# Down projection with sums kept in PSUM banks and block sums in fixed order, and output projection begun in attention for its first column half only

## The chip, the cores and the metric

The kernel runs on one core of one Trainium2 chip. The metric is the device time of one execution in microseconds (us): three executions of the kernel before gave 2621.82, 2611.28 and 2616.64 us, median 2616.64 us. Engines are named as in the profile: PE (TensorE matmul), PEld (its weight loads), DVE (VectorE), ACT (ScalarE), POOL (GpSimd), SP (SyncE, which issues the DMAs).

## The reference, cut to what matters

Two layers on x (1024 rows, 1024 columns, float32). Each is a mixer and a feed-forward part, each with a norm before and a norm after, whose result is added to x.

```
for layer in range(2):
    h = rms_norm(x, norm_mix_pre[layer])
    if layer % 2 == 0:      # FoX heads and MLA heads, outputs concatenated
        m = even_mixer(h, ...)          # ends in  concat(fox_out, mla_out) @ w_out
    else:                   # differential attention with ALiBi
        m = odd_mixer(h, ...)           # ends in  o @ w_out
    x = x + rms_norm(m, norm_mix_post[layer])
    h = rms_norm(x, norm_ffn_pre[layer])
    gate, val = split(h @ w_up)                       # 1024 x 5632
    act = gelu(causal_depthwise_conv3(gate))
    f = (act * val) @ w_down                          # 2816 -> 1024
    x = x + rms_norm(f, norm_ffn_post[layer])
return x
```

`rms_norm(y, g) = y * rsqrt(mean(y*y) + 1e-6) * g`. The two places that the change touches are `@ w_out` (the output projection, contraction over 1024) and `@ w_down` (the down projection, contraction over 2816), with the norm behind each.

## The kernel before, in words

**Numbers.** A float32 operand is cut into a high and a low part (`split`: ACT casts the high part, L121, and DVE or POOL subtracts to get the low part, L122), and each product is three matmuls, high·high, high·low, low·high (`hl`, `mm3`, L142). Every matmul of the kernel but the transposes and a few others has line 142, so groups are told apart by their tiles.

**Order.** The text of the kernel says what is computed. A scheduler, when the kernel is built, fixes each engine's order of instructions; at run time every engine works through its own list in that order and waits on semaphores. The transposed attention output goes to memory (`oT`) and comes back as tiles `ot`. Buffers come from pools with fixed counts: X 14 (128x4x512), Q 18 (128x512), T 6 (128x1024), `raw` 2 (128x1024), WL 8 (128x512); PSUM banks are S 2, mm 2, tr 3, pv 1. A tile has to wait until a buffer of its pool is free.

**Attention and its filler.** Each attention head is a generator (`mla_head`, `diff_head`). `weave` runs a head and between its steps takes steps of a second generator, `dense`, up to a budget for each head (`MLA_DENSE`, `DIFF_DENSE`): matmuls of other work that keep PE busy while DVE, ACT and POOL do the softmax. In the MLA heads of layer 0 `dense` is first the remaining projections of MLA and then `out_first`; in layer 1 it ends in `out_first` too.

**Output projection.** The eight blocks of the contraction (k-blocks) are in two groups. `out_first` does k-blocks 0 to 3, for 8 row blocks m (7 down to 0) and both column halves n: 8 x 2 x 4 x 3 = 192 matmuls a layer, each partial sum copied by ACT to an `opart` buffer. After attention `mixer_end` runs `out_second`: k-blocks 4 to 7, another 192 matmuls, 24 for a row block, and a DVE add with the partial sum for each half (L479). Behind each row block stands the norm: Square with sum on ACT (L202 for the first half, L212 for the second), the gain on POOL (L203, L213), the reciprocal root in small steps on ACT and DVE (L156 to L160), two scalar_tensor_tensor on DVE that add to x (L216, L217), the next norm (L225, L227), transposes on PE (L235), the evacuations of the block sums for the up projection (L506 to L528), and then `ffn_up`.

**Down projection.** `ffn_down` is a 2x2 block product by the Strassen–Winograd scheme with 7 products instead of 8. Each product is `prod(an, bn, ...)`: 11 k-blocks, taken in pairs, x 4 row tiles x 3 = 132 matmuls of 128x512; 7 x 132 = 924 a layer. Of each pair it loads the left block sum (`uraw`; the sums A11, A12, A22, S1 to S4 lie in memory), loads or makes the right one, splits both, and multiplies. Right operands T1 to T4 are differences of the four blocks of the weights: B11 is kept (`dB`), T3 is kept and turned into T2 (`dT`), and `comb` (L684, DVE) makes each where the product needs it, 44 a layer. Each product starts fresh PSUM banks, in the order A11·B11, A12·B21, S3·T3, S2·T2, S1·T1, S4·B22, A22·T4, and the sums between products are DVE adds (L754, L761, L765, L766, L770, L774) and POOL adds (L762) on SBUF tiles `C`. The last product holds back its last 5 k-blocks (`TAIL`) and does them row tile by row tile, so that a row tile is finished every 15 matmuls; behind each comes the norm of its row block (`fin_a`, `post_late`), with no next norm in layer 1.

## Time and profile before

| | |
|---|---|
| median of three runs | 2616.64 us (2611.28 to 2621.82) |
| profiled execution, its own time | 2621.89 us |
| its span in the profile | 2620.1 us |
| granted PE clock, mean | 0.971 |
| PE busy / DVE / ACT / POOL of the span | 94% / 68% / 47% / 50% |
| MLA attention with its filler, layer 0 | 350 to 586 us |
| output projection's second part and norm, layer 0 | 592 to about 700 us |
| down projection, layer 0 | 1095 to 1322 us |
| differential attention, layer 1 | 1370 to 1873 us |
| output projection's second part and norm, layer 1 | 1873 to about 1980 us |
| down projection, layer 1 | 2376 to 2605 us; end of span 2620 us |

Times are us from the start of the span. In the rows of a window view the columns are the stretch, its length, then for PE, PEld, DVE, ACT and POOL the busy time with the number of instructions, then the granted PE clock (1.00 is full), the busy share of the DMA engines and GB/s. A row of waits names the waiting engine and line, what it waited for, and total us, times and the longest. A busy PE is not a PE at its peak, since the ends of matmuls are modelled; counts of matmuls tell more, and a few per cent of their records can be missing.

### The profile page before, as it was taken

The numbers are of one execution on the slowest core, as the hardware profiler recorded it, in microseconds if no ns is written. First come the engines' busy times: TensorE is split into PE (matmuls) and PEld (weight loads), VectorE is DVE, ScalarE is ACT, GpSimd is POOL, SyncE is SP. The second block draws the span as 40 slices with busy tenths as digits, with TensorE's granted clock in tenths as the row PEclk, the third lists the DMA queues.
The fourth block names the chain that finished last, engine by engine and source line by source line (L and its number), as shares of the span: only waits on it lengthen the run. The fifth ranks groups of instructions, "written<-read, shape, count | busy, mean of one in ns | idle before, by whom it ended". The sixth has DMA issues, their size and how long they took to land. (4 is left out here: it accounts for less than half of the span.)

```text
span 2620.1 us, 36572 instructions
## 1 busy us (share of the span) xinstructions
PE 2467.1 (94%) x12326; PEld 2077.1 (79%) x12326; DVE 1768.7 (68%) x3631; ACT 1234.9 (47%) x2465; POOL 1299.1 (50%) x1172
## 2 busy tenths in 40 slices
PE   9999899998799999989989999999969999999897
PEld 7888688776688888878878888987757888887686
DVE  5555788657866666666665676777686666656768
ACT  4455578664433333434445555555454333334443
POOL 3445665435577677731321323322267777776132
PEclk9999999898899999999999999999989999999999
DMA  3332333335222323574542112133442332326545
GB/s 140 91 91 77 113 82 89 97 97 169 75 105 106 108 95 111 181 242 156 173 143 57 59 56 73 57 95 103 146 140 73 109 109 93 108 105 230 184 149 213
DMA packets 172156, 307.78 MB, mean 117 GB/s; under 512 B 16936, under 2 KB 67768, under 8 KB 171968
## 3 DMA queue, kind: packets, MB, share of 16 engines
q1 hardware_dynamic: 171968, 305.44, 35.7%
q8 instruction: 98, 1.61, 0.3%
q14 instruction: 90, 0.74, 0.1%
HBM read 213.84 MB, written 76.85 MB: 111 GB/s over the span
## 5 line engine op out<-in xcount | busy, mean ns | idle before, releaser
L142 PE MATMUL psmm<-hT,whi 128*128 128x512 f32 (+1 forms) x960 | 311.6, 401 | 0.6 <-DVE qb L315 0.5
L122 POOL TENSOR_TENSOR wlo<-wraw,whi 128x512 fp32r<-128x512 f32 (+2 forms) x96 | 130.5, 1367 | 266.4 <-ACT whi L121 241.3
L351 ACT ACTIVATE t<-t,mn 128x896 f32<-128x896 f32 (+7 forms) x256 | 198.9, 777 | 127.7 <-DVE mn L343 121.1
L142 PEld LDWEIGHTS psmm<-hT,whi 128*128 128x128 f32 (+1 forms) x960 | 176.1, 190 | 34.5 <-issue 0.7
L142 PE MATMUL psmm<-hT,wlo 128*128 128x512 f32 (+1 forms) x480 | 190.1, 397 | 0.0
L121 ACT CAST d<-uraw 128x512 fp32r<-128x512 f32 x154 | 91.6, 618 | 140.8 <-DMA uraw<-uS 82.6
L142 PE MATMUL psmm<-wo,ot 128*128 128x512 f32 x576 | 146.8, 397 | 0.0
L380 PE MATMUL pstr<-ident,t 128*128 128x128 f32 x864 | 136.4, 280 | 6.4 <-DVE t L1199 2.1
L122 POOL TENSOR_TENSOR d<-uraw,d 128x512 fp32r<-128x512 f32 x66 | 100.3, 1538 | 84.6 <-ACT d L121 83.7
L142 PE MATMUL psmm<-whi,hT 128*128 128x256 f32 (+1 forms) x576 | 123.0, 301 | 9.1 <-ACT hT L247 4.3
L122 DVE TENSOR_TENSOR d<-wdraw,d 128x512 fp32r<-128x512 f32 x88 | 88.4, 1026 | 58.4 <-ACT d L121 45.3
L142 PEld LDWEIGHTS psmm<-wo,ot 128*128 128x128 f32 x576 | 105.8, 189 | 20.7 <-DVE qb L315 0.2
L610 ACT ACTIVATE y<-gate,cols 128x1024 f32<-128x1024 f32 x44 | 50.8, 1155 | 147.9 <-DVE gate L605 147.9
L142 PE MATMUL pstr<-T,S3h 128*128 128x512 f32 x352 | 112.7, 401 | 5.1 <-DVE B L507 5.1
L142 PE MATMUL psmm<-B,A12h 128*128 128x512 f32 x352 | 110.9, 396 | 5.0 <-DVE B L507 5.0
L380 PEld LDWEIGHTS pstr<-ident,t 128*128 128x128 f32 x864 | 102.9, 145 | 15.9 <-POOL t L902 3.6
L122 DVE TENSOR_TENSOR S2l<-s,S2h 128x512 fp32r<-128x512 f32 x44 | 65.1, 1480 | 74.5 <-ACT S2h L121 74.5
L385 DVE TENSOR_TENSOR ptq<-pstr,ptq 128x512 fp32r<-128x512 f32 (+1 forms) x160 | 99.5, 630 | 23.6 <-ACT ptq L384 19.3
L614 ACT ACTIVATE y<-y,cols 128x1024 f32<-128x1024 f32 x44 | 50.7, 1153 | 135.9 <-DVE y L612 135.9
L603 DVE TENSOR_TENSOR u<-u,psmm 128x512 f32<-128x512 f32 x44 | 29.9, 680 | 117.9 <-PE psmm L142 117.9
L142 PE MATMUL psmm<-B,A11h 128*128 128x512 f32 x352 | 109.3, 390 | 0.0
L142 PE MATMUL psmm<-T,S2h 128*128 128x512 f32 x352 | 108.8, 390 | 0.0
(357 smaller groups left out, 7636.4 us busy)
## 6 DMA issues: line engine op xcount, KB each, us to landing
wdraw<-in_ffn_down_dram SPq DMA_DIRECT2D x60, 512.0 KB, 4.7
wg<-in_ffn_up_dram SPq DMA_DIRECT2D x44, 512.0 KB, 3.4
wv<-in_ffn_up_dram SPq DMA_DIRECT2D x44, 512.0 KB, 3.5
uS<-us SPq DMA_DIRECT2D x88, 256.0 KB, 2.0
uraw<-uS SPq DMA_DIRECT2D x40, 512.0 KB, 4.1
uA<-y SPq DMA_DIRECT2D x66, 256.0 KB, 2.1
ot<-oT SPq DMA_DIRECT2D x64, 256.0 KB, 3.5
uraw<-uA SPq DMA_DIRECT2D x30, 512.0 KB, 4.5
```

The source lines that it names most:

```text
L121: nc.scalar.copy(R(hi), raw)
L122: lo_eng.tensor_tensor(R(lo), raw, hi, ALU.subtract)
L142: ins = nc.tensor.matmul(out, R(l), R(r), start=first and j == 0, stop=last and j == n - 1).ins
L351: nc.scalar.activation(t[:, :W], t[:, :W], AF.Exp, bias=mn, scale=-1.0, accum_out=l)
L380: nc.tensor.transpose(tp[:, c:c + P], pts[qi][:, b * P:(b + 1) * P], ident)
L385: nc.vector.tensor_tensor(R(pl[:, :c]), tp[:, :c], ph[:, :c], ALU.subtract)
L603: nc.vector.tensor_tensor(u2, s1, p6, ALU.add)
L610: nc.scalar.activation(y, gp, AF.Copy, scale=col(2, f))
L614: nc.scalar.activation(y, y, AF.Gelu_apprx_tanh, bias=cb)
```

## The change

1. **Output projection.** `out_first` does only the first column half (96 matmuls, 8 copies). `out_second` does the other half wholly: per row block 12 matmuls for n = 0 as before, and 24 for n = 1, summed in PSUM. It loads and splits the weights of k-blocks 0 to 3 for n = 1 itself and loads `ot` of these k-blocks again. The second half no longer passes a DVE add: Square reads PSUM, and its gain is a DVE multiply from PSUM to `xn`, which takes the place of POOL's L213.
2. **Budgets.** `MLA_DENSE` and `DIFF_DENSE` are lower, most in the last heads.
3. **Down projection.** The products go in the order A11·B11, A12·B21, S2·T2, S1·T1, S3·T3, S4·B22, A22·T4 and sum in PSUM: S2·T2 goes on in the banks of A11·B11, S3·T3 and A22·T4 in those too, and S4·B22 in those of S1·T1. There are 12 DVE evacuations a layer instead of 24 (and 4 gain multiplies from PSUM), 12 ACT copies instead of 8, and no POOL add.
4. **Block sums.** 11 of the 44 subtractions, those that make T2, stay where the product needs them (`comb`); the other 33 are `side` subtractions into the kept tiles, done a pair later, from loads of single 128x512 blocks into WL, each ordered on DVE behind the last split of the pair by a dependency that carries no data. In all 44 as before, with the same bytes.

```diff
-DIFF_DENSE = (29, 31, 28, 32, 30, 30, 28, 25)
+DIFF_DENSE = (27, 29, 26, 30, 28, 27, 24, 20)
-MLA_DENSE = (8, 8, 6, 6, 6, 7, 18, 18)
+MLA_DENSE = (7, 7, 6, 5, 5, 6, 7, 7)
...
-    def mm3(out, prods, first, last):
+    def mm3(out, prods, first, last, more=False):
...
-            ins = nc.tensor.matmul(out, R(l), R(r), start=first and j == 0, stop=last and j == n - 1).ins
+            ins = nc.tensor.matmul(out, R(l), R(r), start=first and j == 0, stop=last and j == n - 1, skip_group_check=more).ins
...
-    def post_late(m, n, src, sse, early, g_post, xi, xq, cut=False):
+    def post_late(m, n, src, sse, early, g_post, xi, xq, cut=False, home=None):
...
-        nc.gpsimd.tensor_tensor(src, src, g_post[n], ALU.mult)
+        if home is None:
+            nc.gpsimd.tensor_tensor(src, src, g_post[n], ALU.mult)
+        else:
+            nc.vector.tensor_tensor(home, src, g_post[n], ALU.mult)
+            src = home
...
     def out_first(w_src, oT, part):
-        w = [wo_quads(w_src, 0, n) for n in range(2)]
+        w = wo_quads(w_src, 0, 0)
...
     def out_second(w_src, oT, part, fin_0, fin_e, fin_a, fin_b, ahead):
-        w = [wo_load(w_src, 4, 0, lambda k: (buf("Q", "woh"), buf("Q", "wol"))), wo_quads(w_src, 4, 1)]
+        lo = buf("X", "wo")
+        w1 = wo_load(w_src, 0, 1, lambda k: (buf("Q", "woh"), lo[:, k, :]))
+        o1 = {7: oT_load(oT, 0, 7, "Q")}
+        w0 = wo_load(w_src, 4, 0, lambda k: (buf("Q", "woh"), buf("Q", "wol")))
+        w1 += wo_quads(w_src, 4, 1)
...
-                r = part[m // 4, n][:, m % 4, :]
-                for k in range(4):
-                    mm3(o, hl(tuple(t[:, k * P:(k + 1) * P] for t in ot[m]), w[n][k]), k == 0, k == 3)
-                nc.vector.tensor_tensor(r, r, o, ALU.add)
+                ks = ((4, 5, 6, 7) if n == 0 else (0, 1, 2, 3, 4, 5, 6, 7) if m == 7 else (4, 5, 6, 7, 0, 1, 2, 3))
+                for k in ks:
+                    src = (ot if k > 3 else o1)[m]
+                    mm3(o, hl(tuple(t[:, (k % 4) * P:(k % 4 + 1) * P] for t in src), w0[k - 4] if n == 0 else w1[k]), k == ks[0], k == ks[-1])
+                if n == 0:
+                    r = part[m // 4][:, m % 4, :]
+                    nc.vector.tensor_tensor(r, r, o, ALU.add)
+                    fin_e(m, 0, r)
+                else:
+                    r = o
...
+            side = dict(B21=((0, 1), b0, 1), T1=((0, 0), b0, 0), B22=((1, 0), t, 1)).get(name)
+            if side:
+                (k, j), dst, first = side
+                b = [buf("WL", "wdside") for _ in range(n)]
+                for i in range(n):
+                    nc.sync.dma_start(b[i], wd[k * NP + g + i, :, j * HALF:(j + 1) * HALF])
+                xy = (b, dst) if first else (t, b)
+                late.append(lambda: [nc.vector.tensor_tensor(d, x, y, ALU.subtract).ins for d, x, y in zip(dst, *xy)])
...
+                for f in side:
+                    for ins in f():
+                        tc.add_manual_dep(ins, last.name, behind, reason="order")
...
+        prod("A11", "B11", x, True)
...
+        prod("A12", "B21", y, True)
...
+        prod("S2", "T2", x, False)
         for t in range(4):
-            nc.scalar.copy(q7[:, t, :], p[t])
+            nc.scalar.copy(u2[:, t, :], x[t])
...
+        prod("S1", "T1", y, True)
...
+        prod("S3", "T3", x, False)
         for t in range(4):
-            tt(c22[:, t, :], q7[:, t, :], p[t], ALU.add)
-            tt(q1[:, t, :], q1[:, t, :], p[t], ALU.add)
+            tt(c22[:, t, :], p5[:, t, :], x[t], ALU.add)
...
+        prod("S4", "B22", y, False, wide=layer == 1)
...
+        prod("A22", "T4", x, False, [lambda t=t: fin_b(t) for t in range(4)], TAIL, layer == 1)
         for t in range(4):
-            tt(q7[:, t, :], q7[:, t, :], p[t], ALU.add)
-            fin_a(4 + t, 0, q7[:, t, :], c22[:, t, :])
+            fin_a(4 + t, 0, x[t], c22[:, t, :], p5[:, t, :])
```

In the rows below a name is the tile's name with the number of its buffer's use; a matmul's row is its output, then weights and moving operand as the profile names them.

PE, the last head of MLA attention in layer 0, before: `psS` and `pspv` are the head's scores and products with V (`mq`, `Vm`, `ptq`), `psmm<-wo,ot` is the filler, the output projection's first part.

```order
L142 MATMUL psmm_6844<-wo_5520,ot_6764 128x512
L142 MATMUL psS_6833<-mq_5341,mq_5154 128x384
L142 MATMUL psS_6833<-mq_5342,mq_5154 128x384
L142 MATMUL psS_6833<-mq_5341,mq_5155 128x384
L142 MATMUL psmm_6844<-wo_5521,ot_6764 128x512
L142 MATMUL psmm_6844<-wo_5520,ot_6766 128x512
L142 MATMUL psmm_6844<-wo_5520,ot_6764 128x512
```

PE in the change: the last filler of the same attention, and what follows it.

```order
L143 MATMUL psmm_7082<-wo_6984,ot_7001 128x512
L143 MATMUL psS_6669<-mq_5522,mq_5335 128x128
L143 MATMUL psS_6669<-mq_5523,mq_5335 128x128
L143 MATMUL psS_6669<-mq_5522,mq_5336 128x128
L143 MATMUL psmm_7082<-woh_6998,ot_7003 128x512
L385 MATMUL pstr_6562<-ident,t_6535 128x128
L385 MATMUL pstr_6562<-ident,t_6513 128x128
```

From there to the end of attention stand 126 rows of the heads without a filler, where before the filler ran into the middle of the last head. The tile `psmm_7082` is the second column half of row block 7, k-blocks 0 to 3: its 12 matmuls are all of the moved work that is still in attention; the other 84 of the 96 stand in `out_second`, 12 behind each row block:

```order
L143 MATMUL psmm_7161<-wo_7025,ot_7045 128x512
L143 MATMUL psmm_7161<-woh_6987,ot_7051 128x512
L143 MATMUL psmm_7161<-wo_6984,ot_7051 128x512
L143 MATMUL psmm_7161<-woh_6987,ot_7053 128x512
L143 MATMUL psmm_7161<-woh_6990,ot_7051 128x512
```

DVE in the down projection of layer 0, where the third product's first pairs are made ready, before (S3·T3): `d<-uraw` and `d<-dT` (L122) are splits that PE waits for, L684 the block sums, L754 the sums of the product before.

```order
L122 TENSOR_TENSOR d_11875<-uraw_11866,d_11874 128x512
L122 TENSOR_TENSOR d_11877<-dT_11322,d_11876 128x512
L684 TENSOR_TENSOR dT_11323<-wdraw_11958,wdraw_11960 128x512 x2
L684 TENSOR_TENSOR dT_11322<-dT_11322,dB_11319 128x512
L684 TENSOR_TENSOR dT_11324<-wdraw_12003,wdraw_12005 128x512 x2
L754 TENSOR_TENSOR C_11327<-C_11326,psmm_11564 128x512
L754 TENSOR_TENSOR C_11327<-C_11326,pstr_11565 128x512
L122 TENSOR_TENSOR d_11849<-uraw_11821,d_11849 128x512
L684 TENSOR_TENSOR dT_11324<-wdraw_12048,wdraw_12050 128x512
L122 TENSOR_TENSOR d_11849<-dT_11322,d_11849 128x512
```

The third product of the change (S2·T2) on the same engine, with the last block sums of the product ahead of it (L700) and the sums L787:

```order
L700 TENSOR_TENSOR dT_11333<-wdraw_12034,dB_11330 128x512 x2
L700 TENSOR_TENSOR dT_11333<-wdraw_12077,dB_11330 128x512
L122 TENSOR_TENSOR d_11867<-uraw_11860,d_11866 128x512
L122 TENSOR_TENSOR d_11869<-dT_11331,d_11868 128x512
L787 TENSOR_TENSOR C_11340<-C_11339,psmm_11574 128x512
L122 TENSOR_TENSOR d_11910<-uraw_11903,d_11909 128x512
L787 TENSOR_TENSOR C_11340<-C_11339,pstr_11575 128x512
L122 TENSOR_TENSOR d_11886<-uraw_11860,d_11886 128x512
```

No block sum stands between the splits of this product any more. The second product, A12·B21, now holds 11 splits, the 11 side subtractions (L726) and the 11 of T2 (L700).

DVE in the last rows of the program, before (L774 is the sum of the last product, L214 to L160 the root, L216 and L217 the additions to x):

```order
L774 TENSOR_TENSOR C_23942<-C_23942,psmm_25511 128x512
L159 TENSOR_SCALAR cvpost_25795<-cvpost_25795,rrpost_25796 128x1
L160 TENSOR_SCALAR rrpost_25796<-cvpost_25795,rrpost_25796 128x1
L216 SCALAR_TENSOR_TENSOR xq_25789<-C_23943,rrpost_25796,xq_25789 128x512
L217 SCALAR_TENSOR_TENSOR xq_25789<-C_23942,rrpost_25796,xq_25789 128x512
```

And in the change, where L217 is the gain multiply from PSUM and L221 and L222 are the additions:

```order
L217 TENSOR_TENSOR C_23968<-psmm_23964,gain_23950 128x512
L219 TENSOR_SCALAR ssl_25834<-ssl_25834,sse_25222 128x1
L158 TENSOR_SCALAR cvpost_25838<-ssl_25834 128x1
L159 RECIPROCAL rrpost_25839<-cspost_25840 128x1
L160 TENSOR_SCALAR cvpost_25838<-cvpost_25838,rrpost_25839 128x1
L161 TENSOR_SCALAR rrpost_25839<-cvpost_25838,rrpost_25839 128x1
L221 SCALAR_TENSOR_TENSOR xq_25832<-C_23969,rrpost_25839,xq_25832 128x512
```

The sum of the last row tile no longer stands in the chain of the row tile ahead of it; the multiply stands in its own.

More of the change, by code (lines that the diff above doesn't have):

```diff
@@ L446, in out_first @@
     def out_first(w_src, oT, part):
[L448 removed]
+        w = wo_quads(w_src, 0, 0)
         for m in range(7, -1, -1):
             ot = oT_load(oT, 0, m)
[L451 to L465 removed]
+            if m // 4 not in part:
+                part[m // 4] = buf("X", "opart")
+            o = bank("mm")
+            for k in range(4):
+                mm3(o, hl(tuple(t[:, k * P:(k + 1) * P] for t in ot), w[k]), k == 0, k == 3)
+                if k < 3:
+                    yield
+            nc.scalar.copy(part[m // 4][:, m % 4, :], o)
+            yield
+    def out_second(w_src, oT, part, fin_0, fin_e, fin_a, fin_b, ahead):
+        lo = buf("X", "wo")
[3 more added lines that the diff above has]
+        w1 += wo_quads(w_src, 4, 1)
         ot = {m: oT_load(oT, 1, m) for m in (7, 6, 5)}
+        o1[6] = oT_load(oT, 0, 6, "Q")
         fin_0(7)
@@ L470, in out_second @@
                 ot[m - 3] = oT_load(oT, 1, m - 3)
+            if m < 7 and m:
+                o1[m - 1] = oT_load(oT, 0, m - 1, "Q")
             if m:
@@ L691, in btiles, with prod @@
                 return b0
-            if name[0] == "B":
-                return bload(int(name[1]) - 1, int(name[2]) - 1, g, n)
-            if name == "T1":
-                b = bload(0, 1, g, n)
-                return comb(b, b, b0, ALU.subtract)
-            if name == "T3":
-                return comb(t, bload(1, 1, g, n), bload(0, 1, g, n), ALU.subtract)
-            if name == "T2":
-                return comb(t, t, b0, ALU.add)
-            b = bload(1, 0, g, n)
-            return comb(b, b, t, ALU.subtract)
-        def prod(an, bn, tags, between=(), tail=0, wide=True):
-            banks = [bank(t) for t in tags]
+            if name in ("T1", "T3"):
+                res = b0
+            elif name == "T4":
+                res = t
+            else:
+                res = bload(*dict(B21=(1, 0), B22=(1, 1), T2=(1, 1))[name], g, n)
+            if name == "T2":
+                return comb(t, res, b0, ALU.subtract)
+            side = dict(B21=((0, 1), b0, 1), T1=((0, 0), b0, 0), B22=((1, 0), t, 1)).get(name)
[6 more added lines that the diff above has]
+                late.append(lambda: [nc.vector.tensor_tensor(d, x, y, ALU.subtract).ins for d, x, y in zip(dst, *xy)])
+            return res
+        def prod(an, bn, banks, start, between=(), tail=0, wide=True):
             between = list(between)
-            held = []
+            held, late = [], []
             def mul(mt, g, t):
@@ L712, in mul @@
                 ms = slice(mt * P, (mt + 1) * P)
-                mm3(banks[mt], hl((ah[:, ms], al[:, ms]), (bh, bl)), g == 0, g == NP - 1)
+                mm3(banks[mt], hl((ah[:, ms], al[:, ms]), (bh, bl)), start and g == 0, g == NP - 1, not start)
             for g0 in range(0, NP, 2):
@@ L729, in prod @@
                     split(ar[:, i * HALF:(i + 1) * HALF], ah, al, nc.vector if bn[0] == "T" else nc.gpsimd)
-                    split(bt[i], bh, bl, nc.gpsimd if an == "A11" and g0 == 0 else nc.vector)
+                    last = split(bt[i], bh, bl, nc.gpsimd if an == "A11" and g0 == 0 else nc.vector)
                     if g0 + i >= NP - tail:
@@ L735, in prod @@
                             mul(mt, g0 + i, t)
+                for f in side:
+                    for ins in f():
+                        tc.add_manual_dep(ins, last.name, behind, reason="order")
                 if between:
                     between.pop(0)()
+            for f in late:
+                f()
             for mt in range(4):
@@ L743, in ffn_down @@
         names = [t for t in ("S", "pv", "mm", "tr") for _ in range(PB[t])]
-        sa, sb_ = names[:4], names[4:]
         tt = nc.vector.tensor_tensor
-        q1, c11, q7, c22 = (buf("X", "C") for _ in range(4))
-        p = prod("A11", "B11", sa)
+        x = [bank(t) for t in names[:4]]
+        q1, c11, u2, p5, c22 = (buf("X", "C") for _ in range(5))
+        prod("A11", "B11", x, True)
         for q in t3q:
@@ L1053, in fin_a @@
         def fin_a(m, n, late, early):
-            post_late(m, n, late, sse[m], early, gpost, 2 * layer, xqs[m])
+            post_late(m, n, late, sse[m], early, gpost, 2 * layer, xqs[m], home=xqs[m][1][:, :HALF])
             pre_norm_a(xqs[m], gpre)
@@ L1073, in fin_e, with fin_a @@
             sse[m] = post_early(n, src, gpost, ostage("o", bufs=2).bitcast(BF16))
-        def fin_a(m, n, late, early):
+        def fin_a(m, n, late, early, home=None):
             xqs[m] = xq_pair("X")
             x_load(m, 2 * layer + 1, xqs[m])
-            post_late(m, n, late, sse[m], early, gpost, 2 * layer + 1, xqs[m], last)
+            post_late(m, n, late, sse[m], early, gpost, 2 * layer + 1, xqs[m], last, home)
             if not last:
```

42 lines of the change are left out of this document (13 added, 29 removed).

## The prediction

> **What bounds the kernel now.** First the page's line of busy times, then windows over the stages, then PE's waits stage by stage.
>
> ```profile
> PE 2467.1 (94%) x12326; PEld 2077.1 (79%) x12326; DVE 1768.7 (68%) x3631; ACT 1234.9 (47%) x2465; POOL 1299.1 (50%) x1172
> ```
>
> PE is busy 2467.1 of the 2620.1 us, and the change neither adds nor removes a matmul. So it can only win some of the 153 us in which PE idles, or lose by adding to them. Where these lie is read stage by stage; the seven stretches that matter:
>
> ```profile
> core 0: us, PE busy (x) PEld busy (x) DVE busy (x) ACT busy (x) POOL busy (x), PEclk, DMA share, GB/s
> 350.00:586.40 236.40, 225.80 (x1397) 199.66 (x1395) 168.84 (x477) 171.92 (x396) 114.49 (x160) 0.97 0.32 88
> 500.00:560.00 60.00, 60.00 (x328) 51.32 (x327) 26.30 (x67) 32.28 (x71) 15.66 (x22) 1.00 0.25 71
> 569.50:586.40 16.90, 15.07 (x110) 13.30 (x108) 13.89 (x43) 13.14 (x32) 7.55 (x11) 1.00 0.30 85
> 1370.00:1862.00 492.00, 475.34 (x2847) 417.93 (x2846) 341.41 (x1095) 258.86 (x569) 135.12 (x188) 0.98 0.25 74
> 617.00:641.00 24.00, 24.00 (x120) 20.12 (x118) 21.59 (x45) 13.52 (x32) 18.37 (x13) 1.00 0.41 141
> 641.00:700.00 59.00, 36.24 (x141) 27.64 (x140) 49.69 (x81) 25.82 (x56) 38.80 (x25) 0.77 0.26 89
> 1922.00:1980.00 58.00, 35.08 (x140) 26.96 (x139) 48.86 (x84) 27.48 (x59) 40.44 (x26) 0.79 0.29 99
> ```
>
> Rows one to four are attention. Both attentions are bound by PE: in MLA's 236.4 us PE idles 10.6 and DVE is busy 71%, in the differential's 492 us 16.7 and 69%; where the output projection fills (500 to 560) PE never stops and DVE has 26.3 of 60. Without filler (569.5 to 586.4) PE is busy 15.07 of 16.9. Rows five to seven are the output projection's second part and the norm: PE first full with DVE at 90%, then, with the projection finished at 641 while the norms run on, PE at 60% for 59 us, in both layers.
>
> ```profile
> 1155.00:1196.00 41.00, 31.39 (x121) 25.04 (x120) 36.39 (x53) 15.78 (x32) 6.06 (x4) 0.88 0.50 170
> 1196.00:1227.00 31.00, 31.00 (x138) 25.67 (x138) 21.60 (x35) 20.44 (x38) 0.00 (x0) 1.00 0.50 165
> 2407.00:2440.00 33.00, 30.41 (x127) 24.68 (x127) 21.17 (x24) 11.85 (x23) 12.04 (x9) 0.95 0.83 292
> 2440.00:2478.00 38.00, 28.92 (x118) 23.12 (x117) 33.91 (x49) 14.55 (x31) 6.15 (x4) 0.87 0.37 128
> PE psS L142 <- DVE d L122: 11.1, 3, 6.1
> ```
>
> These are products of the down projection, 132 matmuls each, and PE's waits for splits in layer 0. S3·T3 (1155 and 2440) takes 41 and 38 us, and DVE is busy 89% of it; its neighbour S2·T2 takes 31 with PE full.
>
> **The change part by part.** The price of a matmul, from the last ones:
>
> ```profile
> 2603.97 0.84 PE L142 MATMUL psmm<-d 128*128 128x512 f32 x3
> 2604.65 0.84 PE L142 MATMUL psmm<-d,d 128*128 128x512 f32 x3
> ```
>
> Three every 0.68 us, 0.227 each.
>
> *Attention.* Of the 96 matmuls a layer that leave `out_first`, the order of PE shows 12 still inside attention, so 84 x 0.227 = 19.0 us of PE work leave each attention. PE bounds it, so at most 19.0 is won. Against that, thinner filler shows waits: of the 126 rows at MLA's end that now have none, the trace already has about 110 matmuls unfilled with 1.8 us lost per 16.9, and the shares of DVE and ACT rise to 169 and 172 of 217 us, under 80%. I charge 6 us a layer for MLA and 5 for the differential one, whose budgets fall by 1 to 5 in each head: three to four waits of 1 to 2 us. **−13 and −14.** Bounds: −19 (no new wait) and −4 (as many us of waits again as PE idles now).
>
> *Output projection's second part.* The 84 matmuls come back here: 24 a row block before, 36 now. PE then needs 36 x 0.227 + about 0.8 for transposes = 9.0 us a row block, 8 x 9.0 = 72 in all where it had 49 (592 to 641). DVE is what the stage waits for now:
>
> ```profile
> PE pstr L235 <- DVE xn L227: 11.1, 3, 7.1
> PE pspv L142 <- ACT B L506: 6.2, 1, 6.2
> 591.81 0.77 PE L142 MATMUL psS<-woh,ot 128*128 128x512 f32 x1 [5.19 <-DMA ot<-oT]
> 674.20 2.39 DVE L227 SCALAR_TENSOR_TENSOR xn<-xr,rrpre,gain 128x1024 f32<-128x1024 f32 x1
> L227 DVE SCALAR_TENSOR_TENSOR xn<-xr,rrpre,gain 128x1024 f32<-128x1024 f32 x8 | 12.6, 1578 | 0.1
> L216 DVE SCALAR_TENSOR_TENSOR xr<-opart,rrpost,xr 128x512 f32<-128x512 f32 x8 | 9.2, 1149 | 0.8 <-POOL opart L203 0.3
> ```
>
> Its row blocks go at 9 us (21.59 busy of 24, 45 instructions), and the chain of the last one ends the stage: PE's waits for `xn` of 11.1 us and for the last evacuation of 6.2. 72 us of PE fit under the 85 us after which the last `xn` is there (591.8 to 676.6 in the rows): the last row block then ends at 592 + 72 = 664, some 12 us of chain behind it (Square, root, additions, the next norm) give 676 as before, and the 59 us stretch with 23 idle is where the 19 us go. **0 in both layers**: hidden by the norms. If that cover fails, rows go at PE's pace with DVE's on top, and up to 19 us a layer come back. The DVE add L479 of 0.68 us becomes a multiply of the same size; POOL loses eight multiplies. Bounds −6 to +8 a layer; the extra loads (`ot` once more, 8 x 2 x 256 KB = 4 MB, and 1 MB of weights that moves here) are some 70 GB/s over 72 us, where DMA shares are 0.26 to 0.41.
>
> ```profile
> 604.77 1.84 DVE L217 SCALAR_TENSOR_TENSOR xr<-opart,rrpost,xr 128x512 f32<-128x512 f32 x1
> 612.38 0.75 DVE L217 SCALAR_TENSOR_TENSOR xr<-opart,rrpost,xr 128x512 f32<-128x512 f32 x1
> 604.78 1.28 POOL L203 TENSOR_TENSOR opart<-opart,gain 128x512 f32<-128x512 f32 x1 [1.25 <-ACT xn L202]
> ```
>
> The same addition takes 1.84 us when a POOL multiply starts beside it and 0.75 alone. By the Trainium skill ("SBUF — State Buffer", "Who interferes with whom") a DVE instruction with two SBUF inputs contends with a GpSimd instruction that reads SBUF, and one with at most one SBUF input does not; the rows agree, and by it every POOL multiply that leaves spares about 1 us, so that the stage would be some 4 us a layer shorter and the whole 8. I keep 0, since POOL still has its other multiply and the block sums to do beside these additions.
>
> *Down projection.* The 44 block sums stay 44, but before, 20 to 26 of them stood in S3·T3 between the splits that PE waits for (order of DVE). Dense, a product is 132 x 0.227 = 29.9 us. S3·T3 is over by 41 − 29.9 = 11.1 in layer 0; A12·B21 and S3·T3 by 3.1 and 8.1 in layer 1: 22.3 in all. Now A12·B21 has 11 splits at 1.0, 22 sums at 0.78 = 28 us of DVE, S1·T1 22 splits at 0.73 and 11 sums = 25, S2·T2 and S3·T3 22 splits and 4 sums = 19.
>
> ```profile
> L122 DVE TENSOR_TENSOR d<-wdraw,d 128x512 fp32r<-128x512 f32 x42 | 41.3, 1002 | 31.4 <-ACT d L121 29.0 <-DMA wdraw<-in_ffn_down_dram 2.4
> L122 DVE TENSOR_TENSOR d<-uraw,d 128x512 fp32r<-128x512 f32 x44 | 31.7, 730 | 18.2 <-ACT d L121 18.2
> L684 DVE TENSOR_TENSOR wdraw<-wdraw,dB 128x512 f32<-128x512 f32 x11 | 8.2, 776 | 0.0
> ```
>
> All under 29.9, A12·B21 barely. I take 17 of 22.3: **−9 and −8**; bounds −22 and −6 for both (A12·B21 late by 8 a layer). The sums moved from SBUF to PSUM banks save DVE 12 x 0.68 = 8 us a layer beside full PE: nothing. At the end of layer 0 PE waits 4.3 us for the next layer's `hT`; four sums and POOL's multiplies fewer in front of it: **−2** (−4 to +1).
>
> ```profile
> PE psmm L142 <- ACT hT L247: 4.3, 1, 4.3
> ```
>
> *The end of layer 1.* After PE's last matmul (2605.5) the last row's sum waits until the chain of the row ahead lets it in:
>
> ```profile
> 2610.19 0.67 DVE L774 TENSOR_TENSOR C<-C,psmm 128x512 f32<-128x512 f32 x1
> 2610.94 0.63 ACT L212 ACTIVATE xq<-C 128x512 f32<-128x512 f32 x1 [0.86 <-DVE C L774]
> 2611.99 1.75 DVE L217 SCALAR_TENSOR_TENSOR xq<-C,rrpost,xq 128x512 f32<-128x512 f32 x1
> 2613.67 0.20 DVE L214 TENSOR_SCALAR ssl<-ssl,sse 128x1 f32<-128x1 f32 x1
> 2614.99 0.75 DVE L216 SCALAR_TENSOR_TENSOR xq<-C,rrpost,xq 128x512 f32<-128x512 f32 x1
> 2615.65 0.75 DVE L217 SCALAR_TENSOR_TENSOR xq<-C,rrpost,xq 128x512 f32<-128x512 f32 x1
> ```
>
> It starts 4.7 us late, and the last addition ends at 2616.4, 10.9 after the last matmul; the output's DMA ends at 2620.1. Now Square (0.63, and 0.19 to read its sum), the multiply (0.68), the root (2613.67 to 2614.99 in the rows, 1.3) and two additions (0.75 each, nothing of POOL's beside them) make about 4.5 us a row; rows come every 15 x 0.227 = 3.4, so the last is up to 2 us late: 5 to 6.5 after the last matmul. **−5** (−7 to −2).
>
> *Sum.* −13 −14 + 0 −9 −8 −2 −5 = −51 on the profiled execution of 2621.9 (span 2620.1 and 1.8 around it): 2571. That execution lies 5.3 above the median 2616.6, so 2565.6 by the median, rounded to **2565**.
>
> **Rivals.** *A, the moved projection is paid back.* For: DVE is at 90% in 617 to 641 and its chain and PE's longer rows may add rather than overlap, since Square and multiply now hold a PSUM bank until both are through. Against: 23 us of idle PE right behind, in each layer. Then attention's 27 come back, 14 to 19 a layer, say 32; the rest is −24: −24 − 27 + 32 = −19, by the median 2597.
>
> *B, A12·B21 is bound by transfers.* It now loads T2's and B12's blocks beside A12 and B21; layer 1's row 2407 to 2440 already shows a DMA share of 0.83 and 3.1 us lost. Some 3 MB more at the 292 GB/s of that row are 10 us a layer, of which about 8 count; single loads of 256 KB have to issue in front of the next `uraw` on SP. Down then gives −1 in place of −17: about 2581. For: DVE's 28 of 29.9 us there. Against: the loads can start in the product before.
>
> *C, slower: the thinner fill lets PE cool.* Place: attention in both layers, at the heads' ends. The trace has such a case:
>
> ```profile
> PE pspv L142 <- DVE ptq L385: 3.3, 1, 3.3
> 480.00:490.00 10.00, 8.68 (x41) 8.20 (x42) 6.71 (x20) 4.79 (x13) 4.17 (x7) 0.66 0.33 96
> 490.00:500.00 10.00, 9.85 (x69) 8.62 (x68) 8.89 (x28) 8.43 (x20) 5.20 (x7) 1.00 0.50 148
> ```
>
> A wait of 3.3 us (to 481.3), and in the 10 us behind it a granted clock of 0.66 and 41 matmuls, then 1.00 and 69. Price: 3.3 and (1 − 0.66) x 10 = 3.4, so 6.7 us. The forecast's 51 are used up from 8 such waits over both layers; ten give −51 + 67 = +16, some 2632. Against: no single wait in the differential attention is over 2.7 us now, and DVE would have 20% of air.
>
> ```profile
> PE psS L142 <- DMA ot<-oT: 2.7, 1, 2.7
> ```
>
> By the Trainium skill ("TensorE: Matmul & The Clock Gate", "What's actually happening") the clock falls to half after an idle window of about 3.4 us and comes back after a busy one of that length. The rows agree as far as 0.66 over 10 us goes, and this speaks for C deciding by long waits only, not by many short ones.
>
> *D, little moves.* PE loses in attention what it is relieved of, the stage behind is hidden, B holds too: only the tail and some 5 of the down projection remain, −10 to −12, about 2605.
>
> **How the numbers follow.** Forecast 0.62, spread 2550 to 2584; A 0.14 (2590 to 2606); B 0.11 (2576 to 2588); D 0.08 (2600 to 2612); C 0.05 (2630 and over). A measurement of this kernel can tell about 0.5% from no change, 13 us, so faster means under 2604. Faster: the forecast, B, most of A and a part of D, 0.85; same 0.10 (rest of A, D, an edge of C); slower 0.05. The range takes in A and leaves out C and most of D, and reaches down by the better ends of attention, down projection and the stage between, −51 − 28: **2538 to 2604**.
>
> **What would show it.** Attention 350 to 586 shorter by 13, 1370 to 1862 by 14, with some 84 matmuls fewer; 592 to 700 and 1873 to 1980 equally long with 84 more and PE nearly full to 660; S3·T3 no longer over 32 us and A12·B21 not over 33; the last addition 5 to 6.5 us behind the last matmul. Wrong: a wait for `xn` as long as before behind a projection that ends 20 us later (A), a DMA share over 0.9 in A12·B21 (B), a clock under 0.9 in attention (C).

## The result, and the profile after

The changed kernel takes 2581.6 us (median of four runs, 2578.5 to 2586.6) where the kernel before took 2619.2 (2611.28 to 2625.39): ratio 0.9857, 95% interval 0.984 to 0.9875, 37.6 us less by the medians. The forecast was 2565, in a range of 2538 to 2604. The profiled execution is the shortest of the four, 2578.5 us with a span of 2576.4; against the profiled execution before the span is 43.7 us shorter.

The page's line of busy times after the change:

```profile
PE 2457.8 (95%) x12326; PEld 2072.2 (80%) x12326; DVE 1754.5 (68%) x3615; ACT 1232.3 (48%) x2457; POOL 1256.7 (49%) x1140
```

PE has the same 12326 matmuls, and its idle time has gone from 153 to 119 us; the other 9 us of the 43.7 are busy time, at a mean granted clock of 0.977 in place of 0.971. To find where, take the first matmul of each part in PE's timeline (start, length, group, what ended the idle time ahead of it), first before, then after:

```profile
1094.74 0.84 PE L142 MATMUL psS<-d,d 128*128 128x512 f32 x3
1873.38 0.76 PE L142 MATMUL psS<-woh,ot 128*128 128x512 f32 x1 [2.73 <-DMA ot<-oT]
2375.62 0.84 PE L142 MATMUL psS<-d,d 128*128 128x512 f32 x3
```

```profile
570.62 0.77 PE L143 MATMUL psS<-woh,ot 128*128 128x512 f32 x1 [6.17 <-DMA ot<-oT]
1077.92 0.84 PE L143 MATMUL psS<-d,d 128*128 128x512 f32 x3
1831.11 0.79 PE L143 MATMUL psS<-woh,ot 128*128 128x512 f32 x1 [1.65 <-DMA ot<-oT]
2335.08 0.84 PE L143 MATMUL psS<-d,d 128*128 128x512 f32 x3
2568.20 0.84 PE L143 MATMUL psmm<-d,d 128*128 128x512 f32 x3
```

`psS<-woh,ot` opens the output projection's second part, `psS<-d,d` the down projection; the last row is its last group in layer 1. With the ends of the down projection (layer 0: 1322.7 before, 1300.8 after; layer 1: 2605.5 and 2569.0), and the stretch between the layers cut at the first product of probabilities with V, they give every part of the span:

| part | before | after | difference | forecast |
|---|---|---|---|---|
| start to second part, layer 0 (attention) | 591.8 | 570.6 | −21.2 | −13 |
| second part to down projection, layer 0 | 502.9 | 507.3 | +4.4 | 0 |
| down projection, layer 0 | 227.9 | 222.9 | −5.0 | −9 |
| passage to layer 1, to its first product with V | 92.0 | 85.2 | −6.8 | −2 |
| from there to the second part, layer 1 (attention) | 458.8 | 445.0 | −13.8 | −14 |
| second part to down projection, layer 1 | 502.2 | 504.0 | +1.8 | 0 |
| down projection, layer 1 | 229.9 | 234.0 | +4.1 | −8 |
| last matmul to end of span | 14.6 | 7.4 | −7.2 | −5 |
| span | 2620.1 | 2576.4 | −43.7 | −51 |

The first row is not all the change's. The same matmul (`psS<-qb,qb` of a head ahead of MLA's, whose budget the change leaves as it was) starts at 345.40 before and at 342.33 after, and in all twelve profiled executions of this document it lies between these two; 3.1 of the 21.2 us are this spread, and 18.1 stand behind that matmul. So the attention windows below start at a common matmul: layer 0, layer 1, and the 20 us that end 5 us ahead of layer 1's second part, first before, then after:

```profile
345.40:586.40 241.00, 230.40 (x1420) 203.54 (x1418) 171.47 (x487) 173.97 (x401) 118.84 (x168) 0.97 0.32 89
1414.63:1873.38 458.75, 438.39 (x2663) 385.97 (x2663) 329.62 (x1083) 243.62 (x546) 127.38 (x182) 0.98 0.26 77
1848.40:1868.40 20.00, 18.17 (x102) 15.05 (x100) 10.83 (x46) 7.71 (x22) 0.32 (x1) 1.00 0.38 132
```

```profile
342.33:564.40 222.07, 210.67 (x1336) 185.37 (x1334) 170.02 (x488) 169.32 (x393) 120.12 (x168) 0.98 0.38 107
1386.06:1831.11 445.05, 424.18 (x2583) 376.61 (x2582) 327.99 (x1076) 240.28 (x538) 122.86 (x182) 0.96 0.28 83
1806.10:1826.10 20.00, 15.90 (x74) 13.60 (x72) 14.14 (x55) 9.46 (x27) 5.41 (x8) 0.60 0.83 277
```

In layer 0 what left is PE work (84 matmul records, 19.7 us), and the idle rest stayed: 10.6 before, 11.4 after, the clock full to the end. In layer 1 the idle rest stayed too (20.4 and 20.9), but PE's busy time fell by only 14.2 us, and its last 20 us, where the filler is thin now, ran at a clock of 0.60 and not 1.00, with 74 matmuls and not 102. No single wait of PE there is over 1.6 us. At this place the kernel before and the run below with the old output projection show 1.00, and all ten with the new one 0.60 to 0.84.

The stage behind, after:

```profile
570.60:646.80 76.20, 75.97 (x348) 62.61 (x348) 54.84 (x114) 34.19 (x81) 33.82 (x23) 0.97 0.56 182
646.80:680.00 33.20, 20.94 (x85) 16.83 (x86) 25.81 (x38) 16.03 (x29) 18.95 (x12) 0.79 0.22 72
```

The second part takes 76 us with PE full to its end; the stretch in which PE used to have holes is 33 us in place of 59.

The down projection is the surprise. The length of each product, by counting off 132 matmuls in PE's timeline (a few records are missing, so a boundary can be off by 0.7 us, a product with PE full shows as 28.6 in place of 29.9, and the last one takes up the rest; before, the third product is S3·T3, the fourth S2·T2, the fifth S1·T1):

| | A11·B11 | A12·B21 | third | fourth | fifth | S4·B22 | A22·T4 |
|---|---|---|---|---|---|---|---|
| before, layer 0 | 31.9 | 29.2 | 43.1 | 30.6 | 28.6 | 28.6 | 36.0 |
| after, layer 0 | 31.5 | 38.3 | 31.3 | 30.6 | 28.6 | 29.2 | 33.4 |
| before, layer 1 | 31.8 | 33.7 | 41.0 | 30.6 | 28.6 | 32.1 | 32.0 |
| after, layer 1 | 31.8 | 38.8 | 37.2 | 29.2 | 29.2 | 35.0 | 32.6 |

```profile
1109.40:1147.80 38.40, 31.43 (x131) 25.22 (x130) 29.88 (x37) 12.29 (x24) 12.93 (x8) 0.91 0.84 291
1147.80:1179.00 31.20, 29.41 (x130) 24.03 (x129) 19.78 (x26) 14.76 (x32) 6.74 (x4) 1.00 0.39 126
2367.00:2405.70 38.70, 32.58 (x129) 25.70 (x127) 28.16 (x35) 12.45 (x25) 12.80 (x9) 0.87 0.89 311
2405.70:2443.00 37.30, 31.74 (x128) 25.69 (x128) 20.09 (x28) 14.54 (x29) 5.44 (x4) 0.91 0.25 80
```

The third product is shorter, as forecast (43.1 to 31.3, and 41.0 to 37.2), and the second is longer by 9 and 5 us. Layer 1's S4·B22 is longer too, by 2 to 3 us, which no run looks into. PE's own rows show how (layer 0, then layer 1; in brackets the wait):

```profile
1121.22 0.50 PE L143 MATMUL psmm<-d,d 128*128 128x512 f32 x1 [1.59 <-ACT d L121]
1127.79 1.22 PE L143 MATMUL psmm<-d,d 128*128 128x512 f32 x2 [5.38 <-DVE d L122]
2384.42 1.22 PE L143 MATMUL psmm<-d,d 128*128 128x512 f32 x2 [5.39 <-DVE d L122]
2412.48 2.07 PE L143 MATMUL psS<-d,d 128*128 128x512 f32 x4 [5.55 <-DVE d L122]
```

Follow the first two back, through SP's queue of issues and ACT's and DVE's timelines of the changed kernel:

```profile
1104.40 7.79 SPq L724 DMA_DIRECT2D wdside<-in_ffn_down_dram  x2
1112.29 0.38 SPq L694 DMA_DIRECT2D wdraw<-in_ffn_down_dram  x1
1112.76 0.38 SPq L742 DMA_DIRECT2D uraw<-uA  x1
1118.98 1.14 ACT L121 CAST d<-uraw 128x512 fp32r<-128x512 f32 x2 [7.59 <-DMA uraw<-uA]
1120.41 2.78 DVE L700 TENSOR_TENSOR dT<-wdraw,dB 128x512 f32<-128x512 f32 x2 [5.92 <-DMA wdraw<-in_ffn_down_dram]
1123.12 1.75 DVE L122 TENSOR_TENSOR d<-wdraw,d 128x512 fp32r<-128x512 f32 x1
1124.79 2.35 DVE L726 TENSOR_TENSOR dB<-wdside,dB 128x512 f32<-128x512 f32 x2
1127.06 1.28 DVE L122 TENSOR_TENSOR d<-wdraw,d 128x512 fp32r<-128x512 f32 x2
```

Two things stand in a row. SP stood from 1104.4 to 1112.2 at a side load; the pool that side loads go to, WL, has eight buffers, and DVE's first side sums, which free two, ran at 1111.4. Behind it waited the third left operand, issued at 1112.76 and cast at 1118.98, 41.1 us behind the down projection's first matmul. And when it had come, DVE first did two sums for T2 (1120.41, 2.78 us) and then, between two splits, two side sums (1124.79, 2.35 us), each of them work that PE does not need yet. Before the change the same load went out at 1127.37 and was cast at 1131.20, 3.8 us later, not 6.2.

So after reading the traces the **theory** was: A12·B21 is long by the order of loads on SP. Its **rivals**: the order of sums and splits on DVE; and the bytes themselves (rival B of the prediction), since the first two products together move some 20 MB in 70 us (38.4 us at 291 GB/s in the row above, and 31.4 at 293 ahead of it).

### The profile page after: what moved, and what is told of

Read it like the earlier page. It is cut to its first block, busy times and chain, and to the rows that moved or that the text cites. A ratio compares the mean times of both kernels' runs of the same rounds, so it can differ in the third digit from the quotient of the medians.

```text
span 2576.4 us, 36603 instructions
## 1 busy us (share of the span) xinstructions
PE 2457.8 (95%) x12326; PEld 2072.2 (80%) x12326; DVE 1754.5 (68%) x3615; ACT 1232.3 (48%) x2457; POOL 1256.7 (49%) x1140
## 3 DMA queue, kind: packets, MB, share of 16 engines
q1 hardware_dynamic: 189344, 313.83, 37.5%
## 4 chain that ended last, share of the span: by engine, by line
PE 38%; DVE 5%; DMA 2%; POOL 2%; issue 2%; ACT 1%; SPq 0%; DVEq 0%; POOLq 0%; ACTq 0%
PE psmm L143 19%; PE psS L143 6%; PE pstr L143 6%; PE pspv L143 5%; PE pstr L385 1%; DVE d L122 1%; DMA wdside<-in_ffn_down_dram 0%; DMA dB<-in_ffn_down_dram 0%; PE pstr L1177 0%; POOL d L122 0%; DVE xq L222 0%; DVE t L348 0%; DVE dT L726 0%; DVE xq L221 0%; DVE t L1230 0%
## 5 line engine op out<-in xcount | busy, mean ns | idle before, releaser
L122 POOL TENSOR_TENSOR wlo<-wraw,whi 128x512 fp32r<-128x512 f32 (+2 forms) x96 | 129.5, 1358 | 260.0 <-ACT whi L121 234.9
L122 POOL TENSOR_TENSOR d<-uraw,d 128x512 fp32r<-128x512 f32 x66 | 103.8, 1593 | 215.5 <-ACT d L121 209.5
L143 PEld LDWEIGHTS psmm<-hT,whi 128*128 128x128 f32 (+1 forms) x960 | 174.0, 188 | 35.9 <-issue 2.5
L143 PE MATMUL psmm<-wo,ot 128*128 128x512 f32 x448 | 123.7, 396 | 0.0
L143 PE MATMUL pstr<-T,A22h 128*128 128x512 f32 x352 | 108.7, 389 | 0.0
L122 DVE TENSOR_TENSOR S2l<-s,S2h 128x512 fp32r<-128x512 f32 x44 | 56.7, 1289 | 74.8 <-ACT S2h L121 74.8
L143 PEld LDWEIGHTS psmm<-hT,wlo 128*128 128x128 f32 (+1 forms) x480 | 90.1, 188 | 20.8 <-POOL wlo L122 1.0
L143 PE MATMUL psS<-B,S4h 128*128 128x512 f32 x336 | 103.7, 390 | 1.1 <-ACT S4h L121 1.1
```

The costliest lines, as they stand in the source:

```text
L122: return lo_eng.tensor_tensor(R(lo), raw, hi, ALU.subtract).ins
L143: ins = nc.tensor.matmul(out, R(l), R(r), start=first and j == 0, stop=last and j == n - 1, skip_group_check=more).ins
```

## The experiments

### Each half of the change alone

Down projection new, output projection and budgets as before:

```diff
-def out_first / out_second / oT_load of the change, MLA_DENSE, DIFF_DENSE of the change
+def out_first / out_second / oT_load of before, MLA_DENSE, DIFF_DENSE of before
```

> The changed down projection (sums in PSUM, new order, side sums) with the output projection and the budgets of before. By the two traces the down projection gives back what it wins (layer 0 shorter by 4 us, layer 1 longer by 4) and only the end of the program (7 us) and the passage between the layers (1.5 us) are shorter: about 8 us below the kernel before. The forecast's own terms for these parts (9 + 8 + 2 + 5) would give 24 us below it.

Output projection and budgets new, down projection as before (both edits are given in words):

```diff
-def ffn_down of the change
+def ffn_down of before
```

> The changed output projection and budgets with the down projection of before. By the two traces attention is 22 us shorter in layer 0 and 21 in layer 1, and the stage behind it takes 4 and 2 us longer: about 36 us below the kernel before. The forecast's terms (13 + 14) would give 27. If the two halves of the change help each other, this and the other half add up to less than the whole.

Measured: the down half 2609.3 us against 2619.9 (ratio 0.9952, 0.9937 to 0.9968), the output half 2593.0 (0.9893, 0.9879 to 0.9908). That is −10.6 and −26.9, together −37.5, as much as the whole change: nothing shows that the halves touch each other. In the down half's trace the two down projections take 225.1 and 236.0 us (227.9 and 229.9 before) and what is won lies in the passage and at the end. The output half stays under the 36 us that were expected of it from the traces, and is right at the forecast's −27; layer 0's attention wins 18.6 there, layer 1's 13.6, the stages behind cost 5.3 and 2.0.

### What makes A12·B21 long

First DVE's order. The T2 sums go behind the last split of A12·B21:

```diff
-                return comb(t, res, b0, ALU.subtract)
+                for d, xx, yy in zip(t, res, b0):
+                    ins = nc.vector.tensor_tensor(d, xx, yy, ALU.subtract).ins
+                    tc.add_manual_dep(ins, mark["A12"].name, behind, reason="order")
+                return t
...
+            mark[an] = last
```

> The changed kernel, with the eleven sums that make T2 ordered on DVE behind the last split of A12.B21. If block sums that stand ahead of splits on DVE make A12.B21 long (it takes 38 us in each layer against 30 dense), its wait of 5.4 us for a split shrinks by 3 us or more in each layer: 6 to 9 us below the changed kernel. If the operands come late from memory, whether by SP's queue or by volume, it stays within 2 us.

2569.2 us, ratio 0.9804 (0.9788 to 0.9819): 12 below the changed kernel, more than either theory said, but not where it was expected. A12·B21 takes 37.6 and 35.9 us, still long; the third product, S2·T2, goes from 31.3 and 37.2 to 29.2 and 28.6:

```profile
2370.70:2406.60 35.90, 31.28 (x131) 25.18 (x130) 28.72 (x36) 14.06 (x27) 12.18 (x8) 0.95 0.86 303
2406.60:2435.20 28.60, 28.60 (x127) 23.66 (x127) 18.86 (x26) 12.82 (x27) 7.17 (x4) 1.00 0.42 143
```

It was not T2's sums themselves that held S2·T2 of layer 1 up, for in the changed kernel these ended at 2397.4. DVE then stood before a sum of the product ahead, with the splits behind it in its list:

```profile
2403.73 0.69 DVE L787 TENSOR_TENSOR C<-C,psmm 128x512 f32<-128x512 f32 x1 [6.29 <-PE psmm L143]
2405.02 0.69 DVE L122 TENSOR_TENSOR d<-dT,d 128x512 fp32r<-128x512 f32 x1
```

With T2's sums moved, the scheduler put four of these splits ahead of that sum (from 2403.16; the sum at 2406.17). No run moved that sum alone.

Then SP's order. A pair's side loads are emitted a pair later, behind the load of the next left operand, and their sums one pair later still:

```diff
+                def load():
+                    b = [buf("WL", "wdside") for _ in range(n)]
+                    for i in range(n):
+                        ins = nc.sync.dma_start(b[i], ...).ins
+                        tc.add_manual_dep(ins, mark[0].name, behind, reason="order")
+                    return lambda: [nc.vector.tensor_tensor(d, x, y, ALU.subtract).ins ...]
...
-                nc.sync.dma_start(ar[...], u_d[layer][an][g0:g0 + n]...)
+                mark[0] = nc.sync.dma_start(ar[...], u_d[layer][an][g0:g0 + n]...).ins
...
-                for f in side:
+                for f in subs:
                     for ins in f():
                         tc.add_manual_dep(ins, last.name, behind, reason="order")
+                subs = [f() for f in side]
```

> The changed kernel, with each pair's side loads ordered on SP behind the load of the next pair's left operand, and their sums one pair later. If SP's queue, which stands for 7.8 us at a side load that waits for a WL buffer, is what brings the left operand late, the operand is there 4 to 5 us earlier and A12.B21 takes 31 to 34 us in each layer: 8 to 14 us below the changed kernel. If the bytes of these two products are too many for the transfers (rival B), or DVE's order is the cause, A12.B21 stays at 37 to 39 us: within 3 us.

2562.2 us, ratio 0.9779 (0.9763 to 0.9796), 19 below the changed kernel. Windows over A12·B21 in layer 0 and 1 and S2·T2 in layer 1, and SP's queue:

```profile
1112.30:1143.50 31.20, 29.86 (x131) 24.05 (x130) 27.96 (x34) 11.39 (x23) 12.72 (x8) 1.00 0.89 305
2361.80:2392.40 30.60, 29.51 (x130) 24.12 (x129) 27.50 (x33) 10.89 (x21) 12.94 (x8) 1.00 0.90 322
2392.40:2428.00 35.60, 31.41 (x130) 25.24 (x130) 21.56 (x30) 16.45 (x34) 6.34 (x4) 0.95 0.39 130
```

```profile
1113.12 0.38 SPq L749 DMA_DIRECT2D uraw<-uA  x1
1113.55 0.46 SPq L726 DMA_DIRECT2D wdside<-in_ffn_down_dram  x1
1114.10 0.38 SPq L749 DMA_DIRECT2D uraw<-uA  x1
```

A12·B21 takes 31.2 and 30.6 us, at 305 and 322 GB/s, and its DVE time of 28 us is just what the forecast had. The kernel moves the same bytes, but some 1.7 MB fewer fall into layer 0's product (31.2 us at 305 GB/s against 38.4 at 291). Counted from the down projection's first matmul (1080.58 here, 1077.92 in the changed kernel), the third left operand is issued at 32.5 us in place of 34.8 and cast at 37.0 in place of 41.1: it goes out 2.3 us earlier and then takes 4.4 us in place of 6.2. DVE's list came out otherwise too: in layer 0 no sums for T2 stand ahead of the split behind that cast any more.

```profile
1117.56 1.15 ACT L121 CAST d<-uraw 128x512 fp32r<-128x512 f32 x2 [3.28 <-DMA uraw<-uA]
1119.26 0.85 DVE L122 TENSOR_TENSOR d<-wdraw,d 128x512 fp32r<-128x512 f32 x1 [3.09 <-ACT d L121]
```

S2·T2 in layer 1 stays long, as it should if that has its own cause. This run moves the side sums too, so the next one moves them without an order on SP: the edit above without the `mark[0]` lines.

> The changed kernel, with the side loads and their sums each one pair later in the program, but no order given on SP: eight side loads still stand ahead of the third left operand there, as many as WL has buffers. If the run before this one won by SP's order, A12.B21 stays at 36 to 39 us and the time within 4 us of the changed kernel (2578 to 2585). If it won because the sums stand one pair later on DVE, this wins as much (about 2562).

2573.4 us, ratio 0.9806 (0.979 to 0.9822). A12·B21 stays at 38.6 and 37.4 us, with a wait of 5.4 and 4.2 us; S2·T2 in layer 1 goes to 30.6. The operand is cast at 40.2 us here, as late as before the edit, and in layer 0 T2's sums again stand ahead of the split. So the sums' place alone doesn't shorten A12·B21, and the order of the loads on SP is needed; how much of the gain is the earlier operand and how much DVE's other list, which came with it, these runs do not part. The time fell by 8 us by the medians and 13 by the ratios, not by at most 4; the traces' two down projections account for 6.7, all of it in layer 1 and most of it S2·T2, which the expectation did not count apart. Both orders together:

> Both orders together: side loads behind the next left operand on SP, T2's sums behind the last split of A12.B21 on DVE. Layer 1's S2.T2 took 35.6 us with the first alone and 28.6 with the second alone; if the two have separate causes, it goes to 29 here and the time to 5 to 8 us below the first alone, 2554 to 2557. If both act on one and the same wait, it stays at 2560 to 2563.

```profile
1111.60:1140.80 29.20, 29.20 (x130) 24.20 (x129) 22.96 (x30) 11.81 (x22) 12.66 (x8) 1.00 0.90 305
2365.70:2397.00 31.30, 29.87 (x131) 24.08 (x130) 27.93 (x34) 12.78 (x24) 12.61 (x8) 1.00 0.89 315
2397.00:2426.70 29.70, 29.58 (x131) 24.16 (x130) 20.26 (x29) 14.83 (x31) 7.16 (x4) 1.00 0.47 155
```

2555.8 us, ratio 0.9742 (0.9727 to 0.9756): faster than both kernels. The down projections take 216.4 and 220.2 us, 21 less than before in all. Not all is gone: S2·T2 in layer 0 takes 33.6.

Last, the bytes: side loads of half the width, in the same number and order; each sum is done in two halves.

```diff
-                    nc.sync.dma_start(b[i], wd[k * NP + g + i, :, j * HALF:(j + 1) * HALF])
+                    nc.sync.dma_start(b[i][:, :HALF // 2], wd[k * NP + g + i, :, j * HALF:j * HALF + HALF // 2])
```

> The changed kernel with side loads of 128x256 in place of 128x512, each sum in two halves of which the second reads the first half's block: the right half of these block sums is not the reference's. 4.3 MB a layer less in all, 1.4 MB of it in A12.B21, the number and the order of the loads on SP kept. If volume bounds A12.B21 (rival B), it falls by the 4 to 5 us that 1.4 MB take at 300 GB/s, and the time by about 9. If SP's wait for a buffer does it, the wait stays and the time falls by 3 us or less.

2567.7 us, ratio 0.9787 (0.977 to 0.9804), by the ratios 18 us below the changed kernel and more than either theory had. A12·B21 goes to 35.6 and 35.1 us, 3 to 4 less, with a wait of 3.6 and 3.9 in place of 5.4; the rest of the gain is in the third product again (29.2 and 29.2); why is not followed up here. In layer 0 the operand is cast at 37.0 us, as early as with SP's order mended, and still PE waits, for DVE does T2's sums and side sums around the first split:

```profile
1117.61 2.71 DVE L700 TENSOR_TENSOR dT<-wdraw,dB 128x512 f32<-128x512 f32 x2 [1.84 <-DMA wdraw<-in_ffn_down_dram]
1120.85 3.58 DVE L728 TENSOR_TENSOR dB<-wdside,dB 128x256 f32<-128x256 f32 x4
```

So an operand that comes 4 us earlier, here by fewer bytes, is worth about 3 of the 8 us, and T2's sums behind the splits with the operand late (the run that moved these sums alone) 1 to 3; with SP's new order, which changed both, PE's waits in the product fell to 1.3 and 1.1 us. Volume has a part in it as long as the loads stand in the wrong order; with the other order the kernel's full bytes fit.

### The budgets

```diff
-MLA_DENSE, DIFF_DENSE of the change
+MLA_DENSE, DIFF_DENSE of before
```

> The changed kernel with the two budget rows of before. The filler has the same matmuls, only earlier in the last heads. If attention won because PE bounds it and 84 matmuls a layer left it, the time stays within 6 us of the changed kernel. If the lower budgets themselves spare waits (attention won 21 us in layer 0 where 84 matmuls are 19.0), it is 8 us or more above it.

2590.1 us against 2623.7 in the same series, ratio 0.9872 (0.9857 to 0.9886); the interval overlaps that of the change: 4 us by the ratios, 8 by the medians, so the run lies between its two theories. In the trace layer 0 is as it was (second part at 571.0), and layer 1's attention takes 453.7 us in place of 445.0; the nine profiles with the lower budgets and the new output projection lie between 441.5 and 446.9. So of layer 1's gain some 8 us hang on the lower budgets; for MLA they don't matter.

### Is the moved projection hidden

The moved matmuls left out:

```diff
-                ks = ((4, 5, 6, 7) if n == 0 else (0, 1, 2, 3, 4, 5, 6, 7) if m == 7 else (4, 5, 6, 7, 0, 1, 2, 3))
+                ks = ((0, 1, 2, 3, 4, 5, 6, 7) if n and m == 7 else (4, 5, 6, 7))
```

> The changed kernel without the moved matmuls: k-blocks 0 to 3 of the second column half are left out for row blocks 6 to 0, so 84 matmuls a layer are missing and the output is not the reference's. If the moved work is hidden by the norms, as the forecast had it, the stretch from the second part to the down projection gets at most 5 us shorter in each layer (about 10 in all, 2570 to 2577). If PE bounds the stage and the moved work is paid back in full (rival A), 19 us in each layer go, 38 in all (about 2543).

2561.4 us, ratio 0.9767 (0.9744 to 0.9789). From the second part to the down projection it takes 497.6 and 499.9 us, 9.7 and 4.1 less than with them. PE then waits for the norms again, as before the change (layer 0):

```profile
PE pstr L240 <- DVE xn L232: 14.2, 3, 11.8
```

So of 19 us of moved work 9.7 cost time in layer 0 and 4.1 in layer 1, the rest is hidden: neither the forecast (at most 5) nor rival A (19), in layer 0 between them and in layer 1 as the forecast had it. That the stage without this work is 5.3 and 2.3 us shorter than before the change is not explained by these runs.

The second gain multiply of this stage back on POOL, behind a copy by DVE:

```diff
-            nc.vector.tensor_tensor(home, src, g_post[n], ALU.mult)
+            if cs.start and not cut and xi in (0, 2):
+                nc.vector.tensor_copy(home, src)
+                nc.gpsimd.tensor_tensor(home, home, g_post[n], ALU.mult)
+            else:
+                nc.vector.tensor_tensor(home, src, g_post[n], ALU.mult)
```

> The changed kernel with the second gain multiply of the stage behind attention back on POOL: DVE copies the PSUM bank to SBUF (0.7 us, as long as the multiply it replaces) and POOL multiplies there. If POOL's reads beside an addition with two SBUF inputs are what makes the addition long, the two additions' mean goes from 0.75 and 0.87 us back to 1.1 to 1.3. If DVE bounds the stage, the time rises by 3 to 5 us a layer, 6 to 10 in all; if PE does, it stays within 3 us.

2579.8 us, ratio 0.9844 (0.9825 to 0.9862): no difference from the change. The additions, in the grouped view of DVE over this stage of layer 0, changed kernel first, then this one:

```profile
L222 DVE SCALAR_TENSOR_TENSOR xr<-xn,rrpost,xr 128x512 f32<-128x512 f32 x8 | 7.0, 874 | 0.0
L221 DVE SCALAR_TENSOR_TENSOR xr<-opart,rrpost,xr 128x512 f32<-128x512 f32 x8 | 6.0, 750 | 0.5
```

```profile
L226 DVE SCALAR_TENSOR_TENSOR xr<-xn,rrpost,xr 128x512 f32<-128x512 f32 x8 | 7.0, 872 | 0.0
L225 DVE SCALAR_TENSOR_TENSOR xr<-opart,rrpost,xr 128x512 f32<-128x512 f32 x8 | 6.9, 861 | 0.5
```

They don't go back to 1.1 to 1.3 us. So it was not this one multiply that made them long; which of POOL's work did is not settled. And the 6 us of DVE time that the two additions have lost in layer 0 since the kernel before (9.2 + 10.1 to 6.0 + 7.0) bring nothing while PE is full.

## Why the prediction was right or wrong, step by step

**Direction and range were right, the size was too large by 16 us**, and the measured 2581.6 is nearly the 2581 of rival B, by luck: on the two profiled executions the forecast's −51 measured −43.7, and the other 9 us lie between these executions and the medians and in the kernel before, whose median a fourth run put up from 2616.6 to 2619.2. Within the 43.7, misses in both directions partly cancel: attention, passage and end won some 15 us more than forecast, the down projections and the stages behind attention lost 22.

The step that failed is the down projection's: "All under 29.9, A12·B21 barely. I take 17 of 22.3". It measured −5.0 and +4.1, together −1. The working counted DVE's busy time for each product (28 us, and 28 to 30 it was) and took it that work of 28 us fits into 30. It asked neither in which order SP would issue the loads nor where among the splits the sums would stand. Rival B named the right product and a right number for the loss, and even the single loads ahead of `uraw` on SP; but it put the cause on bytes, and its sign, a DMA share over 0.9, did not show (0.84 and 0.89). The runs show the product at 31 us with all loads kept, once SP and DVE work in another order; the share of each is not parted. With both orders mended the two down projections win 21 us, close to the 22.3 that the stretches promised.

**Attention, −13 and −14.** In layer 0 the mechanism was right: 84 matmuls left, and nearly everything that they cost came out, 18.1 us of 19.0 behind the first common matmul; the charge of 6 us for new waits was wrong, PE's idle time is 10.6 and 11.4. The 21.2 of the table holds 3.1 us of spread between executions, which is luck. In layer 1 the −13.8 is the forecast's number by another mechanism: the charge of 5 us was for three to four new waits, but idle time grew by 0.5 us, and what was lost went into PE's work at a lower clock. As an estimate, 15.90 us at a clock of 0.60 are worth 6.4 us less than at 1.00. The loss would have been larger with the budgets of before.

**The stage behind, 0 and 0.** Right within its bounds (−6 to +8): +4.4 and +1.8. The step that it rests on, cover by the norms, held for a half to four fifths of the moved work. PE is full to 646.8, where "nearly full to 660" stood, and needed 76 us, not 72.

**Passage −2** was −6.8, **end −5** was −7.2: both gains were taken too small. In the passage PE's idle time fell by 3.5 us and its busy time by 3.2 (clock 0.95 before, 0.97 after). The last addition ends 4.2 us behind the last matmul, not 5 to 6.5:

```profile
2569.80 0.69 DVE L217 TENSOR_TENSOR C<-psmm,gain 128x512 f32<-128x512 f32 x1
2572.46 0.75 DVE L222 SCALAR_TENSOR_TENSOR xq<-C,rrpost,xq 128x512 f32<-128x512 f32 x1
```

The multiply of the last row tile starts 0.8 us after its last matmul, right behind the addition of the row ahead: the allowance of up to 2 us for a late start was not needed.

**Rival C** came in part, though no wait in attention reaches 3 us. Its sign, a clock under 0.9, stands at the place that it named, the heads' end, in layer 1 alone: 0.60 over 20 us. Its price was some 5 us and not 67, and it was not decided "by long waits only": the longest wait there is 1.6 us.

## What to carry to other kernels

When work is moved into a stage, a check that each engine's busy time fits is not enough: write down, for the engine that may not wait, what stands in front of its operand on every in-order queue, the queue that issues the loads among them. A load that waits for a free buffer holds all loads behind it, urgent ones too (7.8 us here); put prefetches behind the next urgent load, and sums that are needed only later behind the splits that are needed now. Filler taken out of a stage that PE bounds was worth nearly its full PE time in layer 0 (18 of 19 us) and less in layer 1 (14), where the thin end ran at a lower clock; and the place it goes to decides how much of that is kept. Read the clock in short windows: a mean of 0.96 over 445 us hid 20 us at 0.60.
